# A pair's two attention heads on half of the array's rows each

## The chip, the cores and the metric

The kernel runs on one core of a Trainium2 chip. The metric is the device time of one execution in microseconds (us). TensorE (PE) multiplies: a matmul holds up to 128 rows of weights (the contraction) and streams the columns of a second operand past them; results add up in PSUM, which has eight banks of 128 x 512 float32. VectorE (DVE), ScalarE (ACT) and GpSimd (POOL) work on tiles of 128 partitions, and SyncE (SP) issues all DMAs here.

## The reference, cut to what matters

One layer of an encoder on 512 tokens of width 1024. The normalised input is projected once into q, k, v (16 heads of 64), z, xBC and dt; attention and a two-way state-space scan (SSD) run beside each other, their results are projected together and added to x, and a gated feed-forward block of width 2816 with a short convolution and a last norm follow.

```python
h = rmsnorm(x, norm1_w)
q, k, v, z, xbc, dt_f, dt_b = jnp.split(h @ w_in, splits, axis=-1)
q, k = partial_rope(q, pos), partial_rope(k, pos)          # heads of 64
attn = dilated_attention(q, k, v)                          # scores q.k over 64 numbers
ssm = ssm_mixer(z, xbc, dt_f, dt_b, ...)
x = x + jnp.concatenate([attn, ssm], -1) @ w_out           # 2048 -> 1024
x = x + conv_gated_mlp(rmsnorm(x, norm2_w), w_up, ...)     # 1024 -> 2 x 2816 -> 1024
return rmsnorm(x, final_norm_w)
```

The three dilated windows of the attention become one softmax over all 512 keys, with the logarithm of how many windows hold a key added to its score.

## The kernel before, in words

All matmuls of large operands are done in float32r with each operand split in a high and a low part: `hi*hi + hi*lo + lo*hi`, three matmuls for one. A job of the input projection (`job_T`) makes 128 output columns for all 512 tokens in 24 matmuls of 512 columns; v, z and the output projection use 256-column pieces.

A q or k job (`prep_q`, `prep_k`) makes a pair of heads: head A on partitions 0 to 63, head B on 64 to 127. Rotary embedding, then the split into high and low. The score matmul wants 128 rows: for each head a q tile with the high part on one half and the low part on the other, and two k tiles, the high part on both halves and the low part on both halves. `move` copies these halves between partitions by DMA: three copies for q, six for k, 72 in all for eight pairs. Then one head and one block of 128 queries take two matmuls of 128 x 512, `q*Kh` and `q*Kl`, which hold all four products (line 941):

```python
PE.matmul(s, qs, Kh[h], start=True, stop=False)
PE.matmul(s, qs, Kl[h], start=False, stop=True)
```

`attention_pair` goes by head and, in a head, by halves of two query blocks: scores in bank `s`, DVE adds the window table and takes the row's extreme, ACT the exponential, PE turns the block over (bank `tr`), ACT and DVE split it (`PT`), and PE multiplies by v (bank `o`).

Jobs of all kinds are woven in program order by `weave` with the times of the table `PLAN`. Then `list_schedule` writes every engine's queue anew: it takes what each instruction needs, a cost for each (`cost`), and from several passes forward and backward the order whose end is earliest in its own reckoning. So neighbours in the source need not be neighbours in an engine's queue. A tag such as `s` names a ring of buffers: `before` in the log makes a new tile wait for the users of the one whose buffer it takes.

The convolution of B, C and x (`conv_silu`) uses the projection's bank `acc` as scratch; there are two such banks. The output projection goes by quarters of 256 columns (`out_quarter`), 192 matmuls of 256 columns each; the first quarter is woven in with the end of attention, the others follow, and then 44 feed-forward jobs (`up_job`) and the last projection.

Of the kernel before, what the change touches and what calls it, by code (L numbers as in the profile page):

```python
# [13 lines left out]
EPS = 1e-6  # L14
SEQ = 512
DM = 1024
LAST = 4
HEAT = (5, 8)
# [69 lines left out]
def cost(name, args, kw):  # L88
# [226 lines left out]
def block_kernel(ctx: ExitStack, tc: tile.TileContext, log, x, w_in, w_out, w_up, w_down,  # L315
# [27 lines left out]
    for side, n in (("left", 16), ("right", 120)):  # L343
# [7 lines left out]
    close_ph = open_pool("work", {"V": 13, "Q": 4, "K": 6, "B": 4, "X": 2, "zs": 3, "C": 2, "S": 6, "xd": 2, "CM": 2,  # L351
                                  "A": 2, "D": 2, "wk": 2, "wkp": 3, "xs": 2, "P": 4, "PT": 4, "m": 4, "half": 4,
                                  "yy": 4})
    PSUM = bass.MemoryType.PSUM
    close_ps = open_pool("psum", {"acc": 2, "trp": 1, "E": 1, "y": 1, "s": 1, "tr": 1, "o": 1}, space=PSUM)
# [120 lines left out]
    def job_T(kind, w, c0, rhs, tag="acc"):  # L476

        wp = unit(kind, w[:, c0:c0 + 128].rearrange("(k p) c -> p k c", p=128), 8, 128)
        acc = PS(tag)
        n = len(rhs)  # L480
        for k, (rh, rl) in enumerate(rhs):
            hi, lo = wp[k]
            PE.matmul(acc, hi, rh, start=(k == 0), stop=False)
            PE.matmul(acc, hi, rl, start=False, stop=False)
            PE.matmul(acc, lo, rh, start=False, stop=(k == n - 1))
        return acc
# [43 lines left out]
    def token_tile(t):  # L530
        xs = []
        for hf in range(2):
            xx = T("K" if 2 * t + hf < 6 else "Q")
            SP.dma_start(xx, x[t * 128:(t + 1) * 128, hf * 512:(hf + 1) * 512])
            xs.append(xx)
        for hf in range(2):
            scr = T("P")
            ACT.activation(scr, xs[hf], AF.Square, accum_out=ssp[:, 2 * t + hf:2 * t + hf + 1])
        s1 = SM([128, 1], "ss1")
        DVE.tensor_add(s1, ssp[:, 2 * t:2 * t + 1], ssp[:, 2 * t + 1:2 * t + 2])  # L540
        r1 = rstd(s1, DM)
        for hf in range(2):
            xx = xs[hf]
            DVE.scalar_tensor_tensor(xx, xx, r1, w1bc[hf], op0=ALU.mult, op1=ALU.mult)
            b = PS(("tr", "trp", "s", "o")[(2 * t + hf) % 4]).rearrange("p (k l) -> p k l", k=4)
# [77 lines left out]
    b = PS("trp")  # L623
# [55 lines left out]
    b = PS("trp")  # L679
# [27 lines left out]
    def ssm_b(g):  # L707
# [3 lines left out]
        b = PS("trp")  # L711
# [16 lines left out]
    def ssm_x(g):  # L728
# [10 lines left out]
        for p2 in range(2):  # L739
            b = PS("trp")  # L740
# [15 lines left out]
    def ssm_states(g, BB, Cn, X):  # L756
# [5 lines left out]
        b = PS("trp")  # L762
# [33 lines left out]
    def ssm_out(g, MS, zs, Cn, X):  # L796
        M, SS = MS
        for p2 in range(2):
# [55 lines left out]
            tb = PS("trp").rearrange("p (i c l) -> p i c l", i=2, c=2)  # L854
# [37 lines left out]
    def move(o, i):  # L892
        SP.dma_start(f(o), f(i))

    def prep_q(t):

        yield {"wkp": 3, "Q": 2}
        qr = rope_rows(job_T("q", w_in, C_Q + t * 128, hT))
        Q = [T("Q", dt=F32R) for _ in range(2)]
        lo = T("wkp", dt=F32R)  # L900
        put("Qh", Q[0], qr)
        on("Ql").tensor_sub(lo, qr, f(Q[0]))
        move(Q[1][A], Q[0][B])
        move(Q[1][B], lo[B])
        move(Q[0][B], lo[A])
        keep(*Q)
        yield 5.2
        return Q

    def prep_k(t):  # L910

        yield {"wkp": 2, "K": 4}
        kr = rope_rows(job_T("k", w_in, C_K + t * 128, hT))
        Kt = [T("K", dt=F32R) for _ in range(4)]
        Kh, Kl = Kt[0::2], Kt[1::2]
# [6 lines left out]
        keep(*Kh, *Kl)  # L922
        yield 5.2
        return Kh, Kl

    def attention_pair(t, Q, KK, vs):
        Kh, Kl = KK
        for h, me in enumerate((A, B)):
            for hf in range(2):
                yield {"P": 2, "PT": 4} | ({"m": 1} if h + hf == 0 else {}) | ({"wkp": 1} if hf == 1 else {})  # L930
                if hf == 0:
                    o = PS("o")
                    if h == 0:
                        m = T("m")
                        keep(m)
                        den = SM([128, 8], "den", 4)
                P = []
                for q in (2 * hf, 2 * hf + 1):
# [4 lines left out]
                    p = T("P")  # L943
                    mn = SM([128, 1], "mn", 4)
                    DVE.tensor_tensor_reduce(p, s, lm[q], -0.125, 3.0e38, ALU.add, ALU.min, mn)
                    ACT.activation(p, p, AF.Exp, scale=-1.0, bias=mn, accum_out=den[:, 4 * h + q:4 * h + q + 1])
                    P.append(p)
                oh = o[:, hf * 256:(hf + 1) * 256]
                for k2 in range(2):
                    b = PS("tr")  # L950
                    for u in range(2):
                        k = 2 * k2 + u
                        for q in range(2):
                            PE.transpose(b[:, u * 256 + q * 128:u * 256 + (q + 1) * 128],
                                         P[q][:, k * 128:(k + 1) * 128], ident)
# [9 lines left out]
                if hf == 1:  # L965

                    tm = T("wkp")
                    cp(tm[me], o[B if h == 0 else A])
                    DVE.tensor_add(m[me], tm[me], o[me])
                    free(Q[h], Kh[h], Kl[h])  # L970
                    if h == 1:
                        free(*vs[t % 2])
                yield 2.6
# [83 lines left out]
    def out_quarter(qr, korder, banks):  # L1057

        c0 = qr * 256
        wo = {}  # L1060
        for n, k in enumerate(korder):
            if k not in wo:
                k0 = k // 4 * 4
                for i, w in enumerate(unit("o", w_out[k0 * 128:(k0 + 4) * 128, c0:c0 + 256]
                                           .rearrange("(k p) c -> p k c", p=128), 4, 256)):
                    wo[k0 + i] = w
            yield k
            mh, ml = parts[k]
            hi, lo = wo[k]
            for t in range(NQ):  # L1070
                o = banks[t // 2][:, (t % 2) * 256:(t % 2 + 1) * 256]
                ts = slice(t * 128, (t + 1) * 128)

                one = PE.matmul(o, mh[:, ts], hi, start=(n == 0 and t % 2 == 0), stop=False).ins
                if n == 0 and t % 2:
                    tc.add_manual_dep(one, opened.name, ISSUE_ORDER, reason="one start opens the bank")
                opened = one
                PE.matmul(o, mh[:, ts], lo, start=False, stop=False)
                PE.matmul(o, ml[:, ts], hi, start=False, stop=(n == 15 and t % 2 == 1))

    obanks = [("acc", "acc"), ("s", "o"), ("E", "y"), ("tr", "trp")]
    first = (0, 1, 2, 3, 8, 9, 10, 11, 4, 5, 12, 13, 6, 14, 15, 7)
    b0 = [PS(tg) for tg in obanks[0]]
    for k in out_quarter(0, first, b0):
# [10 lines left out]
    x2w = []  # L1095
    ss2 = SM([128, 16], "ss2", 1)
    for qr in range(4):
        hf = qr // 2
        if qr == 0:
            banks = b0  # L1100
        else:
            banks = [PS(tg) for tg in obanks[qr]]
            for k in out_quarter(qr, (12, 13, 14, 15, 5, 6, 7, 4, 0, 1, 2, 3, 8, 9, 10, 11), banks):
                if k not in parts:
                    load_mix(k, "hl2")
        cs = slice((qr % 2) * 256, (qr % 2 + 1) * 256)
        for t in range(NQ):
            if qr % 2 == 0:
# [3 lines left out]
            DVE.tensor_add(xx, xx, banks[t // 2][:, (t % 2) * 256:(t % 2 + 1) * 256])  # L1112
            scr = T("fk")
            ACT.activation(scr[:, 0:256], xx, AF.Square, accum_out=ss2[:, 4 * t + qr:4 * t + qr + 1])
        for k in (2 * qr, 2 * qr + 1):
            b = PS("acc" if qr < 3 else ("E", "y")[k % 2])
# [5 lines left out]
            x2w.append((hh, hl))  # L1122
    s2 = SM([128, 4], "s2", 1)
    DVE.tensor_reduce(s2, ss2.rearrange("p (t e) -> p t e", e=4), axis=mybir.AxisListType.X, op=ALU.add)
# [14 lines left out]
    def up_job(i, j):  # L1139
        acc = job_T("u", w_up, i * 128, x2w, tag=ptags[j % 4])  # L1140
# [23 lines left out]
    nss = [0] * NQ  # L1164
    for hf in range(2):
        SP.dma_start(fw[hf], bass.AP(tensor=fnorm.tensor, offset=fnorm.offset + hf * 512,
                                          ap=[[0, 128], [1, 512]]))
    for hf in range(2):
        accs = [PS(("acc", "acc", "s", "o")[t] if hf == 0 else ("E", "y", "tr", "trp")[t]) for t in range(NQ)]
# [12 lines left out]
        for k, t, cs in order:  # L1182
# [11 lines left out]
            xx = x2[t][hf][:, cs]  # L1194
            DVE.tensor_add(xx, xx, o)
# [8 lines left out]
            s3 = SM([128, 1], "s3", 4)  # L1204
            DVE.tensor_add(s3, ss3[:, 4 * t:4 * t + 1], ss3[:, 4 * t + n:4 * t + n + 1])
            r3 = rstd(s3, DM)
# [74 lines left out]
```

## Time and profile before

| | us |
|---|---|
| median of 3 runs | 907.31 (906.53 to 909.83) |
| the profiled execution | 908.54 |
| its span, first to last instruction | 906.8 |
| PE busy | 887.8 |
| DVE busy | 613.3 |
| ACT busy | 467.2 |
| POOL busy | 209.2 |

The granted clock of PE was 0.995 of full over the span. A group of instructions is named by its tiles: `s<-K,Q` is a score matmul, `tr<-ident,P` a transpose, `o<-PT,V` the product with v, `acc<-H,whi` and `acc<-H,wlo` the input projection, `acc<-whi,hl` the output projection, `x2w` the feed-forward input. A matmul's record lasts longer than the time until the next one starts, as matmuls follow each other in a pipeline. Nearly all instructions have line 142, that of the helper which records them, so tiles tell them apart.

### The profile page before, as it was taken

The numbers are of one execution on the slowest core, as the hardware profiler recorded it, in microseconds if no ns is written. First come the engines' busy times: TensorE is split into PE (matmuls) and PEld (weight loads), VectorE is DVE, ScalarE is ACT, GpSimd is POOL, SyncE is SP. The second block draws the span as 40 slices with busy tenths as digits, with TensorE's granted clock in tenths as the row PEclk, the third lists the DMA queues.
The fourth block names the chain that finished last, engine by engine and source line by source line (L and its number), as shares of the span: only waits on it lengthen the run. The fifth ranks groups of instructions, "written<-read, shape, count | busy, mean of one in ns | idle before, by whom it ended". The sixth has DMA issues, their size and how long they took to land.

```text
span 906.8 us, 13520 instructions
## 1 busy us (share of the span) xinstructions
PE 887.8 (98%) x5084; PEld 777.1 (86%) x5084; DVE 613.3 (68%) x1042; ACT 467.2 (52%) x971; POOL 209.2 (23%) x187
## 2 busy tenths in 40 slices
PE   8989999999999999998999999999999999999997
PEld 7968888999799889997899998888888888888886
DVE  5764879975998787888732337777777777623323
ACT  6454578656575765667843434444444444322222
POOL 1063543422542541364244210000000000000000
PEclk9999999999999999999999999999999999999999
DMA  8465332542444643226474324333333333332312
GB/s 257 140 149 138 89 99 93 163 123 70 113 121 117 173 118 99 70 82 200 132 227 157 94 71 116 94 93 93 98 107 98 93 105 105 96 108 75 116 48 93
DMA packets 123986, 105.07 MB, mean 116 GB/s; under 512 B 5776, under 2 KB 101904, under 8 KB 123920
## 3 DMA queue, kind: packets, MB, share of 16 engines
q1 hardware_dynamic: 123920, 104.20, 39.5%
q8 instruction: 40, 0.66, 0.3%
q14 instruction: 26, 0.21, 0.1%
HBM read 88.91 MB, written 5.83 MB: 104 GB/s over the span
## 4 chain that ended last, share of the span: by engine, by line
PE 88%; DVE 4%; POOL 3%; issue 2%; DMA 1%; ACT 1%; SPq 0%; POOLq 0%; ACTq 0%; DVEq 0%
PE acc L142 44%; PE tr L142 13%; PE s L142 12%; PE o L142 6%; PE y L142 5%; PE E L142 4%; PE trp L142 3%; POOL wkp L142 1%; DVE D L142 1%; POOL wlo L142 1%; DMA raw<-in_w_in_dram 1%; DMA mx<-mixA_d 1%; POOL yy L142 0%; DVE wkp L142 0%; DVE yy L142 0%
## 5 line engine op out<-in xcount | busy, mean ns | idle before, releaser
L142 ACT ACTIVATE whi<-raw 128x512 fp32r<-128x512 f32 x256 | 159.8, 630 | 266.0 <-PE acc L142 135.6
L142 DVE TENSOR_TENSOR wlo<-raw,whi 128x512 fp32r<-128x512 f32 x196 | 140.8, 722 | 99.7 <-ACT whi L142 98.7
L142 PE MATMUL acc<-H,whi 128*128 128x512 f32 x512 | 169.9, 403 | 0.0
L142 POOL TENSOR_TENSOR rs_r<-rs_m,half 128x1 f32<-128x1 f32 (+1 forms) x25 | 16.6, 665 | 425.2 <-DVE rs_m L142 425.2
L142 POOL TENSOR_TENSOR wlo<-raw,whi 128x512 fp32r<-128x512 f32 x60 | 81.4, 1362 | 141.8 <-ACT whi L142 123.6
L142 PEld LDWEIGHTS acc<-H,whi 128*128 128x128 f32 x512 | 94.7, 189 | 17.4
L142 PE MATMUL acc<-x2w,whi 128*128 128x512 f32 x352 | 109.1, 390 | 0.0
L142 PE MATMUL acc<-H,wlo 128*128 128x512 f32 x256 | 102.0, 399 | 0.0
L142 PE MATMUL acc<-whi,H 128*128 128x256 f32 x448 | 87.8, 288 | 2.2 <-ACT H L142 1.8
L142 PEld LDWEIGHTS acc<-x2w,whi 128*128 128x128 f32 x352 | 66.0, 188 | 13.6
L142 DVE SCALAR_TENSOR_TENSOR fk<-fk,prm,fk 128x511 f32<-128x511 f32 x88 | 66.1, 751 | 14.1 <-ACT fk L142 12.6
L142 PEld LDWEIGHTS acc<-whi,H 128*128 128x128 f32 x448 | 72.2, 192 | 3.5 <-ACT H L142 2.1
L142 PE MATMUL acc<-x2w,wlo 128*128 128x512 f32 x176 | 68.6, 390 | 0.0
L142 PE MATMUL acc<-wlo,H 128*128 128x256 f32 x224 | 64.6, 288 | 0.0
L142 DVE TENSOR_TENSOR PT<-tr,PT 128x512 fp32r<-128x512 f32 x64 | 43.7, 683 | 20.7 <-ACT PT L142 20.3
L142 PEld LDWEIGHTS acc<-H,wlo 128*128 128x128 f32 x256 | 48.4, 189 | 9.0
L142 PE MATMUL o<-PT,V 128*128 128x256 f32 x256 | 54.5, 296 | 0.9 <-DVE rs_m L142 0.5
L142 ACT ACTIVATE PT<-tr 128x512 fp32r<-128x512 f32 x64 | 38.1, 596 | 33.0 <-PE tr L142 32.5
L142 PE MATMUL s<-x2w,whi 128*128 128x512 f32 x176 | 54.2, 389 | 0.0
L142 PE MATMUL tr<-x2w,whi 128*128 128x512 f32 x176 | 54.2, 389 | 0.0
L142 DVE CUSTOM_DVE_ANT_0 P<-s,lmx 128x512 f32<-128x512 f32 x64 | 43.8, 684 | 13.7 <-PE s L142 11.4
L142 ACT ACTIVATE P<-P,mn 128x512 f32<-128x512 f32 x64 | 46.0, 718 | 13.0 <-DVE mn L142 12.6
(265 smaller groups left out, 2002.7 us busy)
## 6 DMA issues: line engine op xcount, KB each, us to landing
raw<-in_w_in_dram SPq DMA_DIRECT2D x48, 512.0 KB, 3.9
raw<-in_w_up_dram SPq DMA_DIRECT2D x44, 512.0 KB, 3.7
raw<-in_w_down_dram SPq DMA_DIRECT2D x22, 512.0 KB, 3.6
A<-step_d SPq DMA_DIRECT2D x16, 512.0 KB, 5.4
raw<-in_w_out_dram SPq DMA_DIRECT2D x16, 512.0 KB, 3.4
K<-K SPq DMA_DIRECT2D x48, 128.0 KB, 2.5
mx<-mixA_d SPq DMA_DIRECT2D x13, 256.0 KB, 3.5
mx<-mixS_d SPq DMA_DIRECT2D x10, 256.0 KB, 2.6
```

The source lines that it names most:

```text
L142: r = fn(*args, **kw)
```

## The change

q and k keep the layout in which they are made: a high and a low tile each, head A on partitions 0 to 63, head B on 64 to 127. A score is now three matmuls over 64 rows, `Qh*Kh + Qh*Kl + Ql*Kh`, and the source issues the two heads' in turn, each into a bank of its own. All copies between partitions go. `attention_pair` goes by halves of queries first and by head inside; each head's result is merged by halves of 256 columns. The pools change: K 4 instead of 6 tiles, P 6 instead of 4, `s` two banks, and the bank `trp` goes, whose transposes and scratch move to `tr` and `s`. In `cost` a matmul over 64 rows counts half.

Beside that: the output projection goes in three parts (256, 512 and 256 columns) instead of four quarters, the feed-forward jobs take their inputs in another order, and in the tail one step of the last norm is worked out ahead.

```diff
@@ cost
+        if op == "matmul" and args[1].shape[0] == 64:
+            n /= 2
@@ pools
-    "Q": 4, "K": 6, ... "P": 4 ...
+    "Q": 4, "K": 4, ... "P": 6 ...
-    {"acc": 2, "trp": 1, "E": 1, "y": 1, "s": 1, "tr": 1, "o": 1}
+    {"acc": 2, "E": 1, "y": 1, "s": 2, "tr": 1, "o": 1}
@@ q and k
-        put("Kh", Kh[0], kr)
-        on("Kl").tensor_sub(Kl[0], kr, f(Kh[0]))
-        for k0, k1 in (Kh, Kl):
-            move(k1[A], k0[B])
-            move(k1[B], k0[B])
-            move(k0[B], k0[A])
...
+        hi, lo = T(kind, dt=F32R), T(kind, dt=F32R)
+        put(kind + "h", hi, r)
+        on(kind + "l").tensor_sub(lo, r, f(hi))
@@ attention_pair
-                    s = PS("s")
-                    qs = Q[h][:, q * 128:(q + 1) * 128]
-                    PE.matmul(s, qs, Kh[h], start=True, stop=False)
-                    PE.matmul(s, qs, Kl[h], start=False, stop=True)
+                ss = [PS("s") for _ in heads]
+                qs = slice(q * 128, (q + 1) * 128)
+                for i, (a, b) in enumerate(((Qh, Kh), (Qh, Kl), (Ql, Kh))):
+                    for s, me in zip(ss, heads):
+                        PE.matmul(s, a[me][:, qs], b[me], start=(i == 0), stop=(i == 2))
...
-                    cp(tm[me], o[B if h == 0 else A])
-                    DVE.tensor_add(m[me], tm[me], o[me])
+                hs = slice(hf * 256, (hf + 1) * 256)
+                cp(tm[me, 0:256], oh[heads[1 - h]])
+                DVE.tensor_add(m[me, hs], tm[me, 0:256], oh[me])
@@ output projection
-    for qr in range(4):
...
+    for n, (c0, w, tags, ttags) in enumerate(((0, 256, (), "acc"), (512, 512, ("s", "o", "E", "y"), "acc"),
+                                              (256, 256, ("tr", "s"), ("E", "y")))):
@@ feed-forward
-        acc = job_T("u", w_up, i * 128, x2w, tag=ptags[j % 4])
+        acc = job_T("u", w_up, i * 128, x2w, tag=ptags[j % 4], ks=(0, 1, 4, 5, 6, 7, 2, 3))
@@ tail
-            DVE.tensor_add(s3, ss3[:, 4 * t:4 * t + 1], ss3[:, 4 * t + n:4 * t + n + 1])
-            r3 = rstd(s3, DM)
+            DVE.scalar_tensor_tensor(m3, ss3[:, 4 * t + n:4 * t + n + 1], 1.0 / DM, s3, op0=ALU.mult, op1=ALU.add)
+            POOL.tensor_tensor(r3, m3, half[:, 0:1], ALU.pow)
```

The queues show what becomes of the two heads in turn. PE's queue before, the first pair's attention: `s_940` is one query block of head A, `K_761` and `K_762` are its k tiles.

```order
L142 MATMUL s_940<-K_761,Q_663 128x512
L142 MATMUL s_940<-K_762,Q_663 128x512
L142 MATMUL trp_981<-ident,xs_890 128x128
L142 MATMUL acc_1076<-H_101,whi_1068 128x512
L142 MATMUL acc_1076<-H_102,whi_1068 128x512
```

PE's queue now, two query blocks of the second pair. `s_1796` and `s_1797` are heads A and B of one block, `s_1819` and `s_1820` of another; `K_804` and `Q_1120` are the high tiles, `K_805` and `Q_1121` the low ones.

```order
L145 MATMUL s_1796<-K_804,Q_1120 128x512
L145 MATMUL s_1797<-K_804,Q_1120 128x512
L145 MATMUL s_1796<-K_805,Q_1120 128x512
L145 MATMUL s_1797<-K_805,Q_1120 128x512
L145 MATMUL s_1796<-K_804,Q_1121 128x512
L145 MATMUL s_1797<-K_804,Q_1121 128x512
L145 MATMUL o_1544<-PT_1551,V_339 128x256
```

```order
L145 MATMUL s_1819<-K_804,Q_1120 128x512
L145 MATMUL s_1819<-K_805,Q_1120 128x512
L145 MATMUL s_1819<-K_804,Q_1121 128x512
L145 MATMUL y_1814<-xd_1812,B_1215 128x256
L145 MATMUL s_1820<-K_804,Q_1120 128x512
L145 MATMUL s_1820<-K_805,Q_1120 128x512
L145 MATMUL s_1820<-K_804,Q_1121 128x512
```

In the first of these blocks the heads stand in turn, as in the source; in the second head A's three come first, then a matmul over all rows, then head B's three.

The other place is early in PE's queue, where the first B tile is turned over, before and now. `acc_729` and `acc_725` are the end of the same k job, `acc_783` and `acc_772` the job after it, `B_706` the B tile.

```order
L142 MATMUL acc_729<-H_104,whi_725 128x512
L142 MATMUL acc_729<-H_103,wlo_726 128x512
L142 MATMUL trp_712<-ident,B_706 128x128 x4
L142 MATMUL acc_783<-H_101,whi_775 128x512
L142 MATMUL acc_783<-H_102,whi_775 128x512
```

```order
L145 MATMUL acc_725<-H_104,whi_721 128x512
L145 MATMUL acc_725<-H_103,wlo_722 128x512
L145 MATMUL acc_772<-H_101,whi_764 128x512
L145 MATMUL acc_772<-H_102,whi_764 128x512
L145 MATMUL acc_772<-H_101,wlo_765 128x512
```

The four transposes of the B tile moved from row 298 of PE's queue to row 418; the next job's matmuls stand in their place.

## Rows read from the trace of the kernel before

**Rows 1.** The page: busy us and share by engine; shares of the chain.
```profile
PE 887.8 (98%) x5084; PEld 777.1 (86%) x5084; DVE 613.3 (68%) x1042; ACT 467.2 (52%) x971; POOL 209.2 (23%) x187
...
PE 88%; DVE 4%; POOL 3%; issue 2%; DMA 1%; ACT 1%; SPq 0%; POOLq 0%; ACTq 0%; DVEq 0%
```

**Rows 2.** Busy time by stage: stretch, length, engines' busy us, PE clock, DMA.
```profile
100.00:425.00 325.00, 322.87 (x2017) 287.00 (x2015) 272.07 (x475) 212.08 (x495) 137.27 (x120) 1.00 0.42 117
425.00:455.00 30.00, 27.51 (x206) 25.35 (x207) 23.60 (x49) 25.32 (x56) 8.34 (x8) 1.00 0.45 136
455.00:540.00 85.00, 84.48 (x701) 83.74 (x701) 26.84 (x44) 34.59 (x79) 28.22 (x22) 1.00 0.45 143
540.00:890.00 350.00, 350.00 (x1598) 291.67 (x1597) 221.79 (x336) 135.66 (x206) 1.02 (x1) 1.00 0.31 94
```

**Rows 3.** Groups of PE: count, busy us, mean ns, idle us before.
```profile
L142 PE MATMUL s<-K,Q 128*128 128x512 f32 x128 | 44.9, 413 | 0.3 <-DVE mn L142 0.3
```

**Rows 4.** Time line of PE, 105.80 to 109.29: start us, duration us.
```profile
105.80 0.40 PE L142 MATMUL acc<-H,whi 128*128 128x512 f32 x1
106.03 0.39 PE L142 MATMUL acc<-H,wlo 128*128 128x512 f32 x1
...
108.36 0.63 PE L142 MATMUL s<-K,Q 128*128 128x512 f32 x2
108.83 0.40 PE L142 MATMUL acc<-H,whi 128*128 128x512 f32 x1
...
109.29 0.38 PE L142 MATMUL y<-xd,B 128*128 128x256 f32 x1
```

**Rows 5.** Time line of PE in the output projection: 24 matmuls apart.
```profile
530.04 0.28 PE L142 MATMUL trp<-whi,hl 128*128 128x256 f32 x1
...
532.92 0.28 PE L142 MATMUL trp<-whi,hl 128*128 128x256 f32 x1
```

**Rows 6.** Time line of PE in the feed-forward stage: 24 matmuls apart.
```profile
621.40 0.62 PE L142 MATMUL tr<-x2w,whi 128*128 128x512 f32 x2
...
626.85 0.62 PE L142 MATMUL acc<-x2w,whi 128*128 128x512 f32 x2
```

**Rows 7.** Time line: one fill of the bank tr and its readers.
```profile
101.93 0.60 PE L142 MATMUL tr<-ident,P 128*128 128x128 f32 x4
...
102.57 0.60 ACT L142 ACTIVATE PT<-tr 128x512 fp32r<-128x512 f32 x1 [1.60 <-PE tr L142]
...
103.20 0.69 DVE L142 TENSOR_TENSOR PT<-tr,PT 128x512 fp32r<-128x512 f32 x1
```

**Rows 8.** PE's waits, first and last of 14: us, times, longest.
```profile
PE trp L142 <- DVE B L142: 3.5, 1, 3.5
...
PE acc L142 <- DVE hl L142: 0.2, 1, 0.2
```

**Rows 9.** Time line round PE's longest wait.
```profile
61.84 2.70 DVE L142 TENSOR_TENSOR_SCAN D<-A,D 128x1024 f32<-128x1024 f32 x1
62.01 0.60 ACT L142 ACTIVATE acc<-B 128x512 f32<-128x512 f32 x1 [1.89 <-DVE B L142]
...
64.46 0.66 DVE L142 SCALAR_TENSOR_TENSOR B<-acc,B 128x512 f32<-128x512 f32 x1
...
65.18 1.12 PE L142 MATMUL trp<-ident,B 128*128 128x128 f32 x4 [3.49 <-DVE B L142]
```

**Rows 10.** Time line of the tail, last token tile.
```profile
901.34 0.15 DVE L142 TENSOR_TENSOR s<-ss 128x1 f32<-128x1 f32 x1
901.53 0.15 DVE L142 TENSOR_SCALAR rs_m<-s 128x1 f32<-128x1 f32 x1
```

**Rows 11.** The page's DMA issues: KB each, us to landing.
```profile
K<-K SPq DMA_DIRECT2D x48, 128.0 KB, 2.5
```

**Rows 12.** Time line: merging one head's result.
```profile
427.85 0.59 ACT L142 ACTIVATE wkp<-o 64x512 f32<-64x512 f32 x1
...
429.08 0.68 DVE L142 TENSOR_TENSOR m<-wkp,o 64x512 f32<-64x512 f32 x1
```

More of the change, by code (lines that the diff above doesn't have):

```diff
@@ L350, in block_kernel @@
     close_h = open_pool("hT", {"H": 4}, "right")
-    close_ph = open_pool("work", {"V": 13, "Q": 4, "K": 6, "B": 4, "X": 2, "zs": 3, "C": 2, "S": 6, "xd": 2, "CM": 2,
-                                  "A": 2, "D": 2, "wk": 2, "wkp": 3, "xs": 2, "P": 4, "PT": 4, "m": 4, "half": 4,
+    close_ph = open_pool("work", {"V": 13, "Q": 4, "K": 4, "B": 4, "X": 2, "zs": 3, "C": 2, "S": 6, "xd": 2, "CM": 2,
+                                  "A": 2, "D": 2, "wk": 2, "wkp": 3, "xs": 2, "P": 6, "PT": 4, "m": 4, "half": 4,
                                   "yy": 4})
     PSUM = bass.MemoryType.PSUM
-    close_ps = open_pool("psum", {"acc": 2, "trp": 1, "E": 1, "y": 1, "s": 1, "tr": 1, "o": 1}, space=PSUM)
+    close_ps = open_pool("psum", {"acc": 2, "E": 1, "y": 1, "s": 2, "tr": 1, "o": 1}, space=PSUM)
     rings, owner = {}, {}
@@ L474, in unit, with job_T @@
         return out
-    def job_T(kind, w, c0, rhs, tag="acc"):
+    def job_T(kind, w, c0, rhs, tag="acc", ks=range(KO)):
         wp = unit(kind, w[:, c0:c0 + 128].rearrange("(k p) c -> p k c", p=128), 8, 128)
         acc = PS(tag)
-        n = len(rhs)
-        for k, (rh, rl) in enumerate(rhs):
+        for k in ks:
+            rh, rl = rhs[k]
             hi, lo = wp[k]
-            PE.matmul(acc, hi, rh, start=(k == 0), stop=False)
+            PE.matmul(acc, hi, rh, start=(k == ks[0]), stop=False)
             PE.matmul(acc, hi, rl, start=False, stop=False)
-            PE.matmul(acc, lo, rh, start=False, stop=(k == n - 1))
+            PE.matmul(acc, lo, rh, start=False, stop=(k == ks[-1]))
         return acc
@@ L544, in token_tile @@
             DVE.scalar_tensor_tensor(xx, xx, r1, w1bc[hf], op0=ALU.mult, op1=ALU.mult)
-            b = PS(("tr", "trp", "s", "o")[(2 * t + hf) % 4]).rearrange("p (k l) -> p k l", k=4)
+            b = PS(("tr", "s", "s", "o")[(2 * t + hf) % 4]).rearrange("p (k l) -> p k l", k=4)
             for k in range(4):
@@ L622, in block_kernel @@
     cp(dtr, acc)
-    b = PS("trp")
+    b = PS("tr")
     for c in range(4):
@@ L678, in block_kernel @@
         DVE.tensor_scalar(ew[:, d * 64:(d + 1) * 64], ew[:, d * 64:(d + 1) * 64], edge, None, op0=ALU.mult)
-    b = PS("trp")
+    b = PS("tr")
     PE.transpose(b[:, 0:128], ew, ident)
@@ L710, in ssm_b @@
         Bn = conv_silu(job_T("b", w_in, C_X + (8 + g) * 128, hT), 8 + g, "B")
-        b = PS("trp")
+        b = PS("tr")
         for c in range(4):
@@ L739, in ssm_x @@
         for p2 in range(2):
-            b = PS("trp")
+            b = PS("tr")
             for u in range(2):
@@ L761, in ssm_states @@
         keep(M)
-        b = PS("trp")
+        b = PS("tr")
         for c in range(4):
@@ L853, in ssm_out @@
             yield {"m": 1} if g < 3 else {"B": 1}
-            tb = PS("trp").rearrange("p (i c l) -> p i c l", i=2, c=2)
+            tb = PS("tr").rearrange("p (i c l) -> p i c l", i=2, c=2)
             for i in range(2):
@@ L890, in block_kernel @@
     A, B = slice(0, 64), slice(64, 128)
-    def move(o, i):
-        SP.dma_start(f(o), f(i))
-    def prep_q(t):
[L897 to L908, printed above, removed]
@@ new lines, in prep, with attention_pair @@
+    def prep(kind, t):
+        yield {"wkp": 2, kind: 2}
+        r = rope_rows(job_T(kind.lower(), w_in, (C_Q if kind == "Q" else C_K) + t * 128, hT))
+        hi, lo = T(kind, dt=F32R), T(kind, dt=F32R)
+        put(kind + "h", hi, r)
+        on(kind + "l").tensor_sub(lo, r, f(hi))
+        keep(hi, lo)
+        yield 5.2
+        return hi, lo
+    def prep_q(t):
+        return prep("Q", t)
+    def prep_k(t):
+        return prep("K", t)
+    def attention_pair(t, QQ, KK, vs):
+        (Qh, Ql), (Kh, Kl) = QQ, KK
+        heads = (A, B)
+        den = SM([128, 8], "den", 4)
+        for hf in range(2):
+            P = {}
+            for q in (2 * hf, 2 * hf + 1):
+                yield {"P": 2}
+                ss = [PS("s") for _ in heads]
[3 more added lines that the diff above has]
+                        PE.matmul(s, a[me][:, qs], b[me], start=(i == 0), stop=(i == 2))
+                for h, s in enumerate(ss):
@@ L943, in attention_pair @@
                     p = T("P")
+                    keep(p)
                     mn = SM([128, 1], "mn", 4)
@@ L946, in attention_pair @@
                     ACT.activation(p, p, AF.Exp, scale=-1.0, bias=mn, accum_out=den[:, 4 * h + q:4 * h + q + 1])
-                    P.append(p)
-                oh = o[:, hf * 256:(hf + 1) * 256]
+                    P[h, q] = p
+                if q == 3:
+                    free(Qh, Ql, Kh, Kl)
+                yield 1.1
+            for h, me in enumerate(heads):
+                yield {"PT": 4} | ({"m": 1, "wkp": 1} if hf + h == 0 else {"wkp": 1})
+                if hf + h == 0:
+                    m = T("m")
+                    keep(m)
+                if h == 0:
+                    o = PS("o")
+                oh = o[:, h * 256:(h + 1) * 256]
                 for k2 in range(2):
@@ L1055, in load_mix, with out_part @@
         split_mix(k, [m], tag)
-    def out_quarter(qr, korder, banks):
-        c0 = qr * 256
+    def out_part(c0, w, korder, banks, last=0):
         wo = {}
+        u = 512 // w
         for n, k in enumerate(korder):
             if k not in wo:
[L1063 to L1066, printed above, removed]
+                k0 = k // (2 * u) * (2 * u)
+                for i, wk in enumerate(unit("o", w_out[k0 * 128:(k0 + 2 * u) * 128, c0:c0 + w]
+                                            .rearrange("(k p) c -> p k c", p=128), 2 * u, w)):
+                    wo[k0 + i] = wk
@@ L1067, in out_quarter, with out_step @@
             yield k
+            for t in range(NQ):
+                if n < 16 - last:
+                    out_step(t, u, w, banks, [k], wo, n == 0, n == 15)
+        for t in range(NQ if last else 0):
+            out_step(t, u, w, banks, korder[16 - last:], wo, False, True)
+    def out_step(t, u, w, banks, ks, wo, first, end):
+        o = banks[t // u][:, (t % u) * w:(t % u + 1) * w]
+        ts = slice(t * 128, (t + 1) * 128)
+        for k in ks:
             mh, ml = parts[k]
             hi, lo = wo[k]
[L1070 to L1079, printed above, removed]
@@ L1081, in block_kernel @@
-    obanks = [("acc", "acc"), ("s", "o"), ("E", "y"), ("tr", "trp")]
+            one = PE.matmul(o, mh[:, ts], hi, start=first and t % u == 0, stop=False).ins
+            if first and t % u:
+                tc.add_manual_dep(one, opened[0].name, ISSUE_ORDER, reason="one start opens the bank")
+            opened[:] = [one]
+            PE.matmul(o, mh[:, ts], lo, start=False, stop=False)
+            PE.matmul(o, ml[:, ts], hi, start=False, stop=end and k == ks[-1] and t % u == u - 1)
+    opened = []
@@ L1082, in block_kernel @@
     first = (0, 1, 2, 3, 8, 9, 10, 11, 4, 5, 12, 13, 6, 14, 15, 7)
-    b0 = [PS(tg) for tg in obanks[0]]
-    for k in out_quarter(0, first, b0):
+    b0 = [PS("acc"), PS("acc")]
+    for k in out_part(0, 256, first, b0):
         if k in (14, 15):
@@ L1094, in block_kernel @@
     x2 = [[None, None] for _ in range(NQ)]
-    x2w = []
-    ss2 = SM([128, 16], "ss2", 1)
-    for qr in range(4):
[L1098 to L1103, printed above, removed]
+    x2w = [None] * KO
+    ss2 = SM([128, 12], "ss2", 1)
+    rest = (12, 13, 14, 15, 5, 6, 7, 4, 0, 1, 2, 3, 8, 9, 10, 11)
+    for n, (c0, w, tags, ttags) in enumerate(((0, 256, (), "acc"), (512, 512, ("s", "o", "E", "y"), "acc"),
+                                              (256, 256, ("tr", "s"), ("E", "y")))):
+        hf = c0 // 512
+        u = 512 // w
+        banks = b0 if n == 0 else [PS(tg) for tg in tags]
+        if n:
+            for k in out_part(c0, w, rest, banks, LAST_OUT if n == 1 else 0):
                 if k not in parts:
                     load_mix(k, "hl2")
-        cs = slice((qr % 2) * 256, (qr % 2 + 1) * 256)
+        cs = slice(c0 % 512, c0 % 512 + w)
         for t in range(NQ):
-            if qr % 2 == 0:
+            if x2[t][hf] is None:
                 x2[t][hf] = T("x2")
@@ L1111, in block_kernel @@
             xx = x2[t][hf][:, cs]
-            DVE.tensor_add(xx, xx, banks[t // 2][:, (t % 2) * 256:(t % 2 + 1) * 256])
+            DVE.tensor_add(xx, xx, banks[t // u][:, (t % u) * w:(t % u + 1) * w])
             scr = T("fk")
-            ACT.activation(scr[:, 0:256], xx, AF.Square, accum_out=ss2[:, 4 * t + qr:4 * t + qr + 1])
-        for k in (2 * qr, 2 * qr + 1):
-            b = PS("acc" if qr < 3 else ("E", "y")[k % 2])
+            ACT.activation(scr[:, 0:w], xx, AF.Square, accum_out=ss2[:, 3 * t + n:3 * t + n + 1])
+        for k in range(c0 // 128, (c0 + w) // 128):
+            b = PS(ttags if n < 2 else ttags[k % 2])
             for t in range(NQ):
@@ L1121, in block_kernel @@
             DVE.scalar_tensor_tensor(hl, b, col(P_N2, k), f(hh), op0=ALU.mult, op1=ALU.subtract)
-            x2w.append((hh, hl))
+            x2w[k] = (hh, hl)
     s2 = SM([128, 4], "s2", 1)
-    DVE.tensor_reduce(s2, ss2.rearrange("p (t e) -> p t e", e=4), axis=mybir.AxisListType.X, op=ALU.add)
+    DVE.tensor_reduce(s2, ss2.rearrange("p (t e) -> p t e", e=3), axis=mybir.AxisListType.X, op=ALU.add)
     r2 = rstd(s2, DM)
@@ L1168, in block_kernel @@
     for hf in range(2):
-        accs = [PS(("acc", "acc", "s", "o")[t] if hf == 0 else ("E", "y", "tr", "trp")[t]) for t in range(NQ)]
+        accs = [PS(("acc", "acc", "s", "o")[t] if hf == 0 else ("E", "y", "tr", "s")[t]) for t in range(NQ)]
         hs = slice(hf * 512, (hf + 1) * 512)
@@ L1194, in block_kernel @@
             xx = x2[t][hf][:, cs]
+            if hf and cs.stop == 512:
+                sofar[t] = SM([128, 1], "sofar", 4)
+                DVE.tensor_scalar(sofar[t], ss3[:, 4 * t:4 * t + 1], 1.0 / DM, EPS, op0=ALU.mult, op1=ALU.add)
             DVE.tensor_add(xx, xx, o)
```

40 lines of the change are left out of this document (11 added, 29 removed).

## Prediction

> **What bounds the kernel now.** I read the page's engine line and chain first, then a table of busy time by stage, then the time line of TensorE at single matmuls, and last the waits. TensorE (PE) is busy 887.8 of 906.8 us and 88% of the chain that ended last is PE itself; apart from its own weight loads no engine passes 68% [rows 1]. By stage PE stands still for 2.1 us in the attention and scan stage (100 to 425 us), 2.5 us where it runs out (425 to 455), 0.5 us in the output projection and not at all in the feed-forward stage [rows 2]: 5.1 us between 100 us and the tail. So the time is the sum of what PE issues, and an edit is worth what it takes from or adds to that sum. The duration of one matmul in the rows is no price: a score matmul is shown with 413 ns [rows 3], but two of them and the next start lie 0.47 us apart, 0.23 us each, while the record still runs [rows 4]. I price by distances between starts. For 256 columns 24 matmuls take 2.88 us, 0.120 us each [rows 5]; for 512 columns 24 take 5.45 us, 0.227 us each [rows 6].
>
> **The scores.** Before, a head and query block take 2 matmuls over all 128 rows of the array: 16 heads x 4 blocks x 2 = 128 [rows 3], 128 x 0.23 = 29.4 us. After, they take 3 matmuls over 64 rows: 192. A matmul that uses half of the rows still streams 512 columns, so alone I give it the same 0.23 us; the gain needs the other head's matmul on the other half at the same time. Perfect pairing would be 96 intervals, 22.1 us.
>
> Here the order decides. The source issues the heads in turn (A B A B A B), but the list schedule writes PE's queue anew, and in it only 4 of the 32 groups come out as six matmuls in turn, 7 more mostly in turn, and in 21 head A's three stand ahead of head B's three, mostly with other work between. I went through all 192 with one rule: starts follow the order of the queue, a matmul starts when its own half is free, and one over all rows waits for both halves. The score matmuls then form 60 stretches without other work in them, and take 160 intervals: 32 of 96 possible overlaps happen (12 in the four clean groups, 16 in the seven, 4 where an A A A B B B stands unbroken). That is 160 - 128 = 32 intervals more than before: +32 x 0.23 = +7.4 us, all on PE, so on the path.
>
> No row of before shows a matmul on half of the rows, so both ends: with no overlap at all 192 - 128 = 64 intervals, +14.7 us; with all 96 overlaps -32 intervals, -7.4 us. I take the 32 that the order shows.
>
> The Trainium skill (TensorE: Matmul & The Clock Gate, "Part 3: Packing small matmuls — row/col tiling") says that matmuls start and end strictly in program order and are not reordered. By that page the 160 intervals stand; no run here has shown it yet.
>
> **Changes between full and half array.** 60 stretches make 120 changes. Where PE changes between kinds of matmul now, I see no price: from 105.80 to 109.29 us thirteen 512-column matmuls (two of them scores) and four 256-column ones take 3.49 us [rows 4], and 13 x 0.227 + 4 x 0.120 is 3.43. Upper end: if the array had to empty at each change, the overhang of a record over its interval, 0.39 - 0.23 = 0.16 us [rows 4], would be paid 120 times, 19.2 us. I take the value of the nearest row, nothing, and keep the upper end for the range and as a rival.
>
> **Output projection.** Columns 512 to 1023 go from 384 matmuls of 256 columns to 192 of 512: 384 x 0.120 = 46.1 us against 192 x 0.227 = 43.6: -2.5 us, in a stage where PE stands still for only 0.5 us [rows 2].
>
> **The moves.** 72 copies of q and k between partitions go (48 of K [rows 11], 24 of Q) from SP's queue. PE's only wait at the scores is 0.3 us, for DVE [rows 3], so the copies were hidden behind other jobs' matmuls and their going gives nothing by itself. At most the 5.1 us of idle of [rows 2] go with them; at worst nothing changes. I take 0.
>
> **The shared transpose bank.** The bank trp goes, and its 26 fills move to tr beside 72. A fill holds it from 101.93 to 103.89 us, 1.96 us [rows 7], so 98 fills hold it for 192 us of some 400; 0 if the order spreads them, up to a few us if it doesn't. I take 0, since the order already counts the bank's reuse.
>
> **The long stall at 65 us.** PE waits 3.49 us for DVE's B chain at its transposes [rows 8]. In the new order these transposes come over 100 rows later, which looks like a gain. But the next job's first matmul now stands in their place, and it needs the acc bank that the same chain uses: ACT writes acc from B at 62.01 and DVE reads it last from 64.46 to 65.12, behind a 2.70 us scan [rows 9], and DVE's order is unchanged there. The stall stays under another name: 0 (at most 0.5 us, the record of four transposes being 1.12 us here [rows 9] and 0.60 at 101.93 [rows 7]).
>
> **Small ones.** Each head's result is now merged in two halves: 32 ACT copies and 32 DVE adds of 64x256 where there were 16 each of 64x512, at 0.59 and 0.68 us [rows 12]. If a half costs as much as a whole, the worst case, it is +9.4 us on ACT and +10.9 on DVE over the whole attention stage, where they have 212 and 272 us in 325 [rows 2]: beside PE. In the tail one DVE step of 0.15 us and its gap go: from 901.34 to 901.53 [rows 10], -0.2 us on the path. The other orders of k in the feed-forward jobs and of parts in the projection fall where PE has no gap: 0.
>
> **Sum.** +7.4 - 2.5 - 0.2 = +4.7 us. The profiled execution took 908.54 us, 1.74 more than its span; 913.2 there. It lies 1.2 us above the median of the runs shown, 907.31, so the median comes to 912.0 us. This is slower by 0.52%, on the very edge of the 0.5% (4.5 us: 902.8 to 911.8) that a measurement here can tell.
>
> **Rivals.**
> - *The array empties at each change.* The Trainium skill (TensorEngine Tiling (Array Packing), "Key Properties") states that a change of tiling mode drains the engine; it speaks against this change, and [rows 4] can't show it, having one mode only. In this kernel's numbers: 120 x 0.16 = +19.2 us on top, 931 us; half of it, 921.6. For it: a group can then not hide its first weights. Against: no change of kind costs anything visible today. By that page the likeliest time would be this one.
> - *No overlap at all*: +14.7 - 2.7 = +12.0, 919.3 us. The change then doesn't do what it says. For it: no row shows two matmuls streaming at once. Against: nothing either.
> - *The idle time goes.* Without 72 copies in SP's queue and with one score bank more, the 5.1 us of [rows 2] shrink: 912.0 - 4.5 = 907.5, no change. Against: none of the 14 lines of PE's waits, of which the first and the last stand in [rows 8], names a DMA.
> - *Faster: the halves run apart from each other.* If a half that is free takes the other head's matmuls even when three of one head stand in front, up to 96 overlaps happen: -7.4 - 2.7 = -10.1, 897.2 us. The point from which it decides: with 21 overlaps beyond the 32 the sum is nil (21 x 0.23 = 4.8), with 40 it is clearly faster (9.2 - 4.7 = 4.5). Against: in every row here starts keep the queue's order, and with a full-array matmul between A A A and B B B nothing can move up.
>
> **How the numbers follow.** The order's own count with free changes, with a spread of 4 us for stalls that the new order moves: 0.42 (0.18 no change, 0.24 slower). A price at the changes: 0.25, slower. No overlap: 0.08, slower. Idle time goes: 0.11 (0.10 no change, 0.01 faster). More overlap: 0.14 (0.13 faster, 0.01 no change). Faster 0.14, same 0.29, slower 0.57. The likeliest case alone is 908 to 916 us. The range is 901 to 930 us: below it lies most of the case of full overlap (about 0.1), above it the full price at every change (about 0.08).
>
> **What would show it.** In the profile after: in a clean group of six, the second score matmul starts within some 0.02 us of the first and the third 0.23 us later; in an A A A B B B group starts lie 0.23 us apart. PE's busy time rises to about 892 us with about the same idle. A gap of about 0.1 us or more at the first and last score matmul of a stretch would show the price of a change. Starts of B beside A where three of A stand in front, or PE idle below 15 us, would make the forecast wrong on the fast side; clean groups 1.4 us long on the slow side.

## The result, and the profile after

The changed kernel takes 932.36 us (median of 4 runs, 929.93 to 932.66); the kernel before, run beside it, 907.75. The ratio is 1.0263, with a 95% interval from 1.0236 to 1.0289: slower by 24.6 us. Forecast were 912.0 us and a range of 901 to 930. The direction was right, the size was not.

The profiled execution took 929.93 us with a span of 928.2. Its page, busy time by engine and shares of the chain, to be read against [rows 1]:

```profile
PE 910.1 (98%) x4956; PEld 766.2 (83%) x4956; DVE 624.7 (67%) x1054; ACT 465.0 (50%) x979; POOL 208.3 (22%) x187
...
PE 92%; DVE 3%; POOL 1%; ACT 1%; issue 1%; DMA 1%; SPq 0%; POOLq 0%; ACTq 0%
```

PE is busy for 22.3 us more than before with 128 fewer matmuls, and stands still for 18.1 us where it stood still for 19.0 (span less busy time). So the loss is in time that counts as busy: not a new wait, but longer distances between matmuls. By stage, with the columns of [rows 2]:

```profile
100.00:425.00 325.00, 324.43 (x1940) 270.96 (x1938) 256.39 (x446) 200.89 (x476) 127.29 (x114) 1.00 0.29 83
425.00:455.00 30.00, 29.61 (x195) 23.97 (x195) 26.04 (x57) 20.53 (x51) 8.64 (x6) 1.00 0.25 80
455.00:560.00 105.00, 102.96 (x667) 92.10 (x665) 47.15 (x80) 51.83 (x112) 37.70 (x31) 1.00 0.48 153
560.00:910.00 350.00, 350.00 (x1598) 291.57 (x1597) 223.86 (x343) 134.79 (x212) 1.02 (x1) 1.00 0.31 94
```

In the attention and scan stage PE gets through 1940 matmuls in 325 us, where it had 2017 in the same length [rows 2]; the feed-forward stage is as it was, 1598 matmuls in 350 us. The loss sits where the scores are. Time line of PE round one score stretch in the changed kernel (start us, duration us), to be read against [rows 4]:

```profile
97.95 0.62 PE L145 MATMUL acc<-H,whi 128*128 128x512 f32 x2
98.51 0.96 PE L145 MATMUL s<-K,Q 64*128 64x512 f32 x3
99.39 0.50 PE L145 MATMUL acc<-H,wlo 128*128 128x512 f32 x1
99.73 0.40 PE L145 MATMUL acc<-H,whi 128*128 128x512 f32 x1
```

From 97.95 to 99.73 six matmuls of 512 columns start (two `whi`, three scores, one `wlo`), 1.78 us. At the distance of [rows 6], 0.227, six take 1.36. So this stretch costs 0.42 us more than its matmuls, for its two changes of mode. Two of the places can be seen in these rows: the first score starts 0.56 us after two matmuls that normally take 0.46 (+0.10), and the matmul after the one that follows the scores starts 0.34 us later instead of 0.23 (+0.11). The other two lie inside the 0.88 us of the scores. The second and third score by themselves:

```profile
98.84 0.62 PE L145 MATMUL s<-K,Q 64*128 64x512 f32 x2
```

The second starts 0.33 us behind the first (98.51 to 98.84, +0.10), and from it two scores take 0.55 us to the next full matmul (98.84 to 99.39, +0.09). So each change leaves some 0.1 us before the first matmul of the new mode and some 0.1 us behind it.

A rival reading is that every half-row matmul is slow by itself. A stretch of one score, in which the full matmul follows at once, speaks against it:

```profile
104.39 0.49 PE L145 MATMUL s<-K,Q 64*128 64x512 f32 x1
104.81 0.50 PE L145 MATMUL acc<-H,whi 128*128 128x512 f32 x1
```

One score takes 0.42 us to the next full matmul, three take 0.88: the two more cost 0.23 us each, as full matmuls do. The extra time belongs to the stretch and not to its matmuls.

The weight loads (PEld) of the same stretch:

```profile
97.72 0.42 PEld L145 LDWEIGHTS acc<-H,whi 128*128 128x128 f32 x2
98.51 0.52 PEld L145 LDWEIGHTS s<-K,Q 64*128 64x128 f32 x3 [0.36 <-issue]
99.39 0.19 PEld L145 LDWEIGHTS acc<-H,wlo 128*128 128x128 f32 x1 [0.36 <-issue]
99.50 0.42 PEld L145 LDWEIGHTS acc<-H,whi 128*128 128x128 f32 x2
```

Within one mode a load runs ahead: that of the two `whi` matmuls of 97.95 starts at 97.72. At a change it doesn't: it starts together with its matmul (98.51 and 98.51, 99.39 and 99.39), after PEld stood still for 0.36 us, for which the profile names no releaser ("issue").

A second thing shows where three scores of head A and three of head B stand unbroken in the queue, A A A B B B:

```profile
93.14 0.60 PE L145 MATMUL tr<-ident,B 128*128 128x128 f32 x4
93.67 0.97 PE L145 MATMUL s<-K,Q 64*128 64x512 f32 x6
94.57 0.73 PE L145 MATMUL acc<-H,whi 128*128 128x512 f32 x2
```

From the first of the six to the next matmul it is 0.90 us, as for the three above (98.51 to 99.39, 0.88). Six took the time of three, although all of A's stood ahead of B's. The scores as a group, against [rows 3], and the first and last of the nine lines of PE's waits, against [rows 8]:

```profile
L145 PE MATMUL s<-K,Q 64*128 64x512 f32 x192 | 51.2, 433 | 0.0
```

```profile
PE acc L145 <- DVE B L145: 3.5, 1, 3.5
...
PE o L145 <- ACT PT L145: 0.3, 1, 0.3
```

The long stall stayed under another name, as forecast; PE is shown with no idle time before a score (0.0).

### The profile page after: what moved, and what is told of

Read it like the earlier page. It is cut to its first block, busy times and chain, and to the rows that moved or that the text cites. A ratio compares the mean times of both kernels' runs of the same rounds, so it can differ in the third digit from the quotient of the medians.

```text
span 928.2 us, 13152 instructions
## 1 busy us (share of the span) xinstructions
PE 910.1 (98%) x4956; PEld 766.2 (83%) x4956; DVE 624.7 (67%) x1054; ACT 465.0 (50%) x979; POOL 208.3 (22%) x187
## 4 chain that ended last, share of the span: by engine, by line
PE 92%; DVE 3%; POOL 1%; ACT 1%; issue 1%; DMA 1%; SPq 0%; POOLq 0%; ACTq 0%
PE acc L145 46%; PE s L145 16%; PE tr L145 14%; PE o L145 6%; PE y L145 6%; PE E L145 4%; DVE D L145 1%; POOL wkp L145 1%; DMA raw<-in_w_in_dram 1%; DVE K L145 1%; DVE PT L145 0%; SPq L145 0%; POOL wlo L145 0%; ACT PT L145 0%; DVE C L145 0%
## 5 line engine op out<-in xcount | busy, mean ns | idle before, releaser
L145 POOL TENSOR_TENSOR wlo<-raw,whi 128x512 fp32r<-128x512 f32 x60 | 87.2, 1460 | 155.2 <-ACT whi L145 150.5
L145 PE MATMUL acc<-whi,H 128*128 128x256 f32 x448 | 92.0, 293 | 1.6 <-ACT H L145 1.2
L145 POOL TENSOR_TENSOR r<-m,half 128x1 f32<-128x1 f32 x4 | 2.2, 549 | 359.2 <-DVE m L145 359.2
```

The costliest lines, as they stand in the source:

```text
L145: r = fn(*args, **kw)
```

## The experiments

Three theories stood against each other. Theory 1: a change between full and half array costs PE about 0.20 us, whatever stands before it; 120 of them are 24 us. Theory 2: a change is free, and the excess comes from what came with it (one transpose bank, two score banks, the new order). Theory 3: the excess is score intervals alone, counted in strict queue order. All times below are medians of a kernel's runs. The kernel before took 908.76 us beside the kernels of experiments 1, 3 and 4, and 908.81 beside those of experiment 2. 0.228 us stands for the distance of two matmuls of 512 columns (0.227 in [rows 6]).

**1. The same order on all rows.** The changed kernel with every queue as it is; only the rows that the score matmuls take are others. In `cost` they still count half, so that the list schedule writes the same order: the records of PE, DVE, ACT and POOL follow each other in the two traces alike.

```diff
-                        PE.matmul(s, a[me][:, qs], b[me], start=(i == 0), stop=(i == 2))
+                        PE.matmul(s, a[:, qs], b, start=(i == 0), stop=(i == 2))
```

> The changed kernel with every engine's queue as it is, but its 192 score matmuls take all 128 rows of q and k instead of 64 (each score is then the sum over both heads, so this part of the computation is another one). No change of array mode is left, and no overlap. Theory 1 (120 changes cost 24 us): 932.4 - 24 + (192 - 152) x 0.228 = 917.5 us. Theory 2 (the excess comes from the banks, the waits or the new order, which are the same here): 932.4 + 9.1 = 941.5 us. PE's idle time should stay at some 18 us by both.

Measured: 917.22 us (916.69 to 918.49), ratio to the kernel before 1.0091 (1.0064 to 1.0118). The page's engine line:

```profile
PE 898.6 (98%) x4956; PEld 778.3 (85%) x4956; DVE 625.7 (68%) x1054; ACT 464.9 (51%) x979; POOL 210.0 (23%) x187
```

As theory 1 said to 0.3 us, and 24 below theory 2: with the order, the banks and the pools unchanged, the kernel gets 15.1 us faster although its scores now take 192 intervals instead of 152. The price of a change follows: (932.36 - 917.22 + 40 x 0.228) / 120 = 0.202 us. PE's idle time is 17.3 us (915.9 - 898.6), about the same. In 100 to 425 us PE now gets through 2008 matmuls, where the changed kernel had 1940.

**2. A half matmul where nothing else happens.** In the kernel before, one extra matmul in the middle of each of the 44 feed-forward jobs: over all rows, over half of them, a pair of halves, and over all rows with 64 columns of weights. The cut shows the four variants under each other; a kernel has one of them, the pair's has the second and third, and what keeps them in place in the queue is left out (`...`).

```diff
             last = PE.matmul(acc, lo, rh, start=False, stop=(k == n - 1)).ins
+            if kind == "u" and k == 3:
+                z = PS("E")
+                x = PE.matmul(z, hi, rh, start=True, stop=True).ins                   # full
+                x = PE.matmul(z, hi[0:64], rh[0:64], start=True, stop=True).ins       # half
+                x = PE.matmul(PS("y"), hi[64:128], rh[64:128], ...).ins               # the pair's second
+                x = PE.matmul(z[0:64], hi[:, 0:64], rh, start=True, stop=True).ins    # 64 columns
...
```

> The kernel before with one more 512-column matmul over all 128 rows in the middle of each of the 44 feed-forward jobs, where PE never stands still; its result goes to a bank that nobody reads. Both theories: 44 x 0.228 = 10.0 us more, 917.7 us. It is the base for the next two.

> As the kernel with a full matmul inserted, at the same 44 places, but the inserted matmul takes rows 0 to 63 only: 88 changes of array mode, nothing else. Theory 1 (0.20 us a change): 44 x (0.228 + 0.40) = 27.6 us more than before, 935.3 us. Theory 2 (no price): 917.7 us, as with the full one. If the price comes from what surrounds the scores in the attention stage (banks, waits), it must be missing here.

> As the kernel with a half matmul inserted, with a second one behind it on rows 64 to 127, into another bank. Theory 1 with halves that run at the same time: the second costs nothing, 935.3 us as with one half. If the halves followed each other: 44 x 0.228 = 10.0 us more, 945.3 us. If a price is paid also between the halves, 0.1 us or more each: 940 us or more.

> As the kernel with a full matmul inserted, but its weights have 64 columns instead of 128 (all 128 rows, 64 rows of output). If only a change of the rows costs: 917.7 us. If any change of the array's shape costs the same: 935.3 us. Theory 1 as it stands says nothing of columns; I lean to 917.7.

| inserted 44 times | us | ratio to the kernel before |
|---|---|---|
| full | 919.48 (916.13 to 923.46) | 1.0121 (1.0086 to 1.0156) |
| half | 937.26 (934.55 to 937.61) | 1.0308 (1.0286 to 1.0331) |
| pair of halves | 937.91 (935.94 to 939.70) | 1.0322 (1.0296 to 1.0347) |
| full, 64 columns of weights | 919.50 (918.72 to 922.13) | 1.0129 (1.0104 to 1.0154) |

Half against full: 17.8 us for 88 changes, 0.202 us each: the price of experiment 1 again, far from attention, its banks and its waits. By the intervals of the ratios each of the two prices is only good to some 0.03 or 0.04 us, so that both come to 0.202 is closer than these medians can tell. The time lines are sharper: over all 44 places the four distances round the inserted matmul sum to 1.304 us with the half one and 0.904 with the full one on average, 0.400 us a place, 0.200 a change. At one place, with the full matmul inserted (`E<-x2w,whi`):

```profile
623.29 0.39 PE L142 MATMUL acc<-x2w,wlo 128*128 128x512 f32 x1
623.52 0.39 PE L142 MATMUL E<-x2w,whi 128*128 128x512 f32 x1
623.75 0.61 PE L142 MATMUL acc<-x2w,whi 128*128 128x512 f32 x2
624.20 0.39 PE L142 MATMUL acc<-x2w,wlo 128*128 128x512 f32 x1
```

With the half one, matmuls and then weight loads:

```profile
621.99 0.39 PE L142 MATMUL s<-x2w,wlo 128*128 128x512 f32 x1
622.31 0.50 PE L142 MATMUL E<-x2w,whi 64*128 64x512 f32 x1
622.74 0.72 PE L142 MATMUL s<-x2w,whi 128*128 128x512 f32 x2
623.30 0.39 PE L142 MATMUL s<-x2w,wlo 128*128 128x512 f32 x1
```

```profile
621.77 0.19 PEld L142 LDWEIGHTS s<-x2w,wlo 128*128 128x128 f32 x1
622.31 0.18 PEld L142 LDWEIGHTS E<-x2w,whi 64*128 64x128 f32 x1 [0.35 <-issue]
622.74 0.30 PEld L142 LDWEIGHTS s<-x2w,whi 128*128 128x128 f32 x2 [0.24 <-issue]
```

Four matmuls take 0.91 us with the full one (623.29 to 624.20) and 1.31 with the half one (621.99 to 623.30). The 0.40 us lie in three distances: 0.32 to the half matmul where 0.23 stood (+0.09), 0.43 behind it (+0.20), 0.56 for the next two instead of 0.45 (+0.11). So a change costs some 0.09 us before the first matmul of the new mode, and some 0.11 behind it. The loads say the same as in the changed kernel: none of the first loads of a mode runs ahead, and the first matmul of a mode has a record that is 0.11 us longer (0.50 instead of 0.39). That the second 0.11 is this load is a reading of the rows and not shown; the load was not varied by itself.

The pair and the 64 columns, one place each:

```profile
614.47 0.39 PE L142 MATMUL acc<-x2w,wlo 128*128 128x512 f32 x1
614.79 0.50 PE L142 MATMUL E<-x2w,whi 64*128 64x512 f32 x1
614.79 0.50 PE L142 MATMUL y<-x2w,whi 64*128 64x512 f32 x1
615.22 0.73 PE L142 MATMUL acc<-x2w,whi 128*128 128x512 f32 x2
```

```profile
621.22 0.39 PE L142 MATMUL acc<-x2w,wlo 128*128 128x512 f32 x1
621.45 0.40 PE L142 MATMUL E<-x2w,whi 128*64 128x512 f32 x1
621.68 0.62 PE L142 MATMUL acc<-x2w,whi 128*128 128x512 f32 x2
```

The second half starts with the first and adds next to nothing, in the rows and in the median (0.65 us, inside both spreads). With half of the columns the distances stay at 0.23: next to no price is seen (the four distances take 0.920 us on average over the 44 places, 0.904 with the full matmul).

**3. Groups kept together.** The changed kernel, with the six score matmuls of a group glued in the list schedule, in two orders.

```diff
+    for g in log.glue:                       # the first of a group waits for what any of it waits for
+        for i, j in zip(g, g[1:]):
+            for d, lag in deps[j].items():
+                if d not in g:
+                    deps[g[0]][d] = max(deps[g[0]].get(d, -1e9), lag)
+            deps[j][i] = 0                   # and the next of a group is taken first
...
-                for i, (a, b) in enumerate(((Qh, Kh), (Qh, Kl), (Ql, Kh))):
-                    for s, me in zip(ss, heads):
+                for s, me in zip(ss, heads):                                    # A A A B B B only
+                    for i, (a, b) in enumerate(((Qh, Kh), (Qh, Kl), (Ql, Kh))):
```

> The changed kernel, with the six score matmuls of a group (one query block, both heads, A B A B A B) kept together in PE's queue: 32 stretches instead of 60, so 64 changes between full and half array instead of 120, and 96 intervals instead of 152. Theory 1 (a change costs about 0.20 us on PE, whatever stands before it): 932.4 - 56 x 0.20 - 56 x 0.228 = 908.4 us, up to 4 us more if the group now waits for its second bank. Theory 2 (a change costs nothing; what the forecast missed is something else, such as the one transpose bank): only the intervals go, 932.4 - 12.8 = 919.6 us. Theory 3 (the forecast's strict queue order, all of the excess being score intervals): 160 - 96 = 64 intervals fewer, 932.4 - 14.6 = 917.8 us.

> As the kernel with glued groups, but head A's three matmuls stand ahead of head B's three. If the two halves of the array run apart from each other, B's first starts beside A's first, a group takes 3 intervals and the time is that of the glued kernel with the heads in turn (theory 1: 908.4 us). If starts keep the order of the queue, as the forecast counted, a group takes 5 intervals: 32 x 2 x 0.228 = 14.6 us more than with the heads in turn (923 us).

Measured: 914.55 us with the heads in turn (913.51 to 917.49), ratio 1.0066 (1.0040 to 1.0092); 910.81 with A A A B B B (909.86 to 914.46), ratio 1.0034 (1.0017 to 1.0051). One group of each, in turn and then A A A B B B:

```profile
98.07 0.96 PE L145 MATMUL s<-K,Q 64*128 64x512 f32 x6
98.96 0.50 PE L145 MATMUL acc<-H,whi 128*128 128x512 f32 x1
```

```profile
97.15 0.97 PE L145 MATMUL s<-K,Q 64*128 64x512 f32 x6
98.05 0.50 PE L145 MATMUL acc<-H,whi 128*128 128x512 f32 x1
```

0.89 and 0.90 us, which are also the medians over the 32 groups of each kernel: the order of the heads inside a group makes no difference, where strict queue order wanted 0.46 us more for each group. The two halves take their work from the queue apart from each other.

The second kernel agrees with theory 1 (908.4, up to 4 more). The first misses it by some 2 us and is not at theory 2 or 3 either, so its median by itself decides nothing. Its profiled execution, the slowest of its four (917.49 us), has PE waiting 5.3 us for PT at the one transpose bank (1.3 in the changed kernel) and 2.6 us for a parameter load at the start, and behind such waits a stretch at the lower clock:

```profile
430.00:435.00 5.00, 2.89 (x17) 2.11 (x17) 5.00 (x7) 4.57 (x12) 1.46 (x1) 0.97 0.16 27
435.00:440.00 5.00, 4.69 (x19) 3.61 (x20) 4.08 (x10) 1.82 (x4) 0.00 (x0) 0.50 0.32 95
```

(Columns of [rows 2].) After 2.89 us of work in 5 the granted clock is 0.50 of full, 1.2 GHz, and PE starts 19 matmuls in 5 us. How much of the first kernel's 3.7 us over the second comes from this in every run stays open; the intervals of the two ratios overlap, and the list schedule also ordered the rest of the two differently.

**4. The other edits alone.** The kernel before with the output projection in three parts (`out_part`), the order of k in the feed-forward jobs and the shorter tail; the last part uses the banks tr and trp.

```diff
-                                              (256, 256, ("tr", "s"), ("E", "y")))):
+                                              (256, 256, ("tr", "trp"), ("E", "y")))):
```

> The kernel before with only the other edits of the change: output projection in three parts, order of k in the feed-forward jobs, the shorter tail; scores and moves as before. By the forecast's terms 907.7 - 2.5 - 0.2 = 905.0 us. Rival: the wider part needs four banks at once and its first matmuls wait for them, which takes the gain back: 907 us or more.

Measured: 906.19 us (904.08 to 907.23), ratio 0.9964 (0.9949 to 0.9978). The output projection and the feed-forward stage, to be read against [rows 2]:

```profile
455.00:540.00 85.00, 84.79 (x527) 75.99 (x526) 31.19 (x45) 36.26 (x75) 30.68 (x23) 1.00 0.49 152
540.00:890.00 350.00, 350.00 (x1593) 291.55 (x1592) 221.35 (x337) 132.26 (x204) 0.00 (x0) 1.00 0.31 94
```

PE stands still for 0.2 us in 455 to 540 and not at all behind it: the wider part waits for nothing. 2.6 us are won (2.0 to 4.6 by the interval), 2.7 were forecast. It is the fastest version here, by 0.4%.

## Why the prediction was wrong

- **Changes between full and half array, priced at nothing: the step that failed.** Each costs 0.202 us, found twice by different means: 120 x 0.202 = 24.2 us. It was priced from a row in which PE changes between sizes and kinds of matmul, all of them on 128 rows [rows 4]; that row holds no change of mode, and being the nearest one didn't make it a witness. The upper end failed too: 0.16 us, a record's overhang, supposed that only the emptying of the array can be lost. About 0.09 us is lost before the first matmul of the new mode, and 0.11 behind it, where its weights had not been loaded ahead. The sign that the prediction named for a price is there, a gap of 0.1 us at the ends of a stretch, and PE's busy time rose to 910.1 us, not 892. The rival that named this mechanism had a chance of 0.25 and said 931 us; it came within 1.4 us, partly by luck: 0.16 us a change is 5.0 us too little in all, and against that it kept 8 intervals too many (1.8 us) and nothing for the few us that moves, banks and merges gave back. The range ended at 930 us, one below that rival's price, so it left out the very case that came.
- **Scores, +32 intervals: half right.** The queue was read rightly (60 stretches), but the rule that starts keep the queue's order was wrong. Between the halves it doesn't hold, so a stretch takes as many intervals as its fuller half has matmuls: 152 instead of 160 in all, 24 x 0.228 = +5.5 us instead of +7.4. The rival of halves that run apart was right in its mechanism but not in its result: with a full matmul between A A A and B B B nothing can move up, as said, and only 40 of 96 overlaps happen. The Trainium skill (TensorE: Matmul & The Clock Gate, "Part 3: Packing small matmuls — row/col tiling") has matmuls start and end strictly in program order; the A A A B B B groups here disagree (six in 0.90 us), and the measurement decides.
- **Output projection -2.5 and tail -0.2: right** as a sum, by experiment 4 (-2.6 us for both).
- **Moves, shared bank, merges, all at nothing: right to a few us.** The kernel of experiment 1 holds them and no change of mode. From the kernel before, its sum is +64 x 0.228 - 2.7 = +11.9 us; it measured +8.5 (5.8 to 10.7 by its interval). PE's idle time fell by 1.7 us there. So by this sum they gave back a little together, one to six us; which of them did is open.
- **The long stall: right.** 3.5 us before and after, under another name.

The corrected sum is 5.5 + 24.2 - 2.7 = +27.0 us; measured were +24.6 (21.4 to 26.2 by the interval). The difference is the few us just named, seen once more; it is no second witness for them.

Why the idea loses at all: a block of both heads takes 4 x 0.228 = 0.91 us on the full array. On halves, perfectly grouped, it takes 3 x 0.228 + 2 x 0.202 = 1.09. Even 32 unbroken groups lose 32 x 0.18 = 5.6 us, or 2.9 with the projection's gain; the A A A B B B kernel measured +2.1. By the same numbers two blocks in one stretch would be at break-even (6 x 0.228 + 0.40 = 1.77 against 1.82); that needs four score banks where there are two, and was not tried.

## What to carry to other kernels

Before splitting the array's rows, count in PE's queue how often it goes from full to half and back: each stretch of half-row matmuls must save more than its two changes cost, here 0.40 us, nearly two matmuls of 512 columns. So keep such matmuls together, and look at the queue that is issued, not at the source. And where no row of the profile shows an operation's kind, the nearest row is a bound on nothing: give the range the price of everything that normally runs ahead there, the weight load too.

## What the runs showed that was not expected

- A change between 128 and 64 rows costs 0.202 us of PE time (17.8 us for 88, 24.2 us for 120), the same behind 512-column matmuls of the feed-forward stage and in the mixed work of attention. The Trainium skill (TensorEngine Tiling (Array Packing), "Key Properties") states that a change of mode drains the engine; the rows agree that something is lost (some 0.09 us before the first matmul of the new mode), and show that more of it comes after that matmul (some 0.11 us).
- A change between 128 and 64 columns of weights has no price that these runs can see: 919.50 us against 919.48.
- Matmuls on the two halves overlap fully, and need not stand in turn: a pair costs what one costs (937.91 against 937.26 us, inside both spreads), and A A A B B B takes 0.90 us where A B A B A B takes 0.89.
